# Expert weights in tiles of 2 MB, 16 KB to a partition, in a pool laid over the first part's pages

## The chip, the cores and the metric

The kernel runs on one core of a Trainium2 chip. The metric is the device time of one execution, in microseconds. The kernel before took 1446.26 us (median of three runs, 1442.34 to 1448.63). The profile is of one more execution.

## What is computed

One layer of a hybrid block over 256 latent tokens of width 1024 with a context of 256 tokens. The first part is a modulated norm, one input projection, a Fourier branch, a gated delta-rule branch, and the merge of both (`w_gdn_out`, then `w_merge_out`). The second part is a mixture of 32 experts, four of them per token, and a final norm:

```
p = u @ w_in                                   # first part, per token
x = x + g1 * ((ga * ya + gb * (yb @ w_gdn_out)) @ w_merge_out)
h2 = modulate(rmsnorm(x, norm2_g), sh2, sc2)
top 4 of 32 experts by h2 @ w_router + b_router
gate = min(h @ w_gate[e] + b_gate[e], 7);  up = clip(h @ w_up[e] + b_up[e], -7, 7)
y = ((up + 1) * gate * sigmoid(1.702 * gate)) @ w_down[e] + b_down[e]
x = x + g2 * sum over the token's experts of weight * y
out = rmsnorm(x, final_norm_g)
```

Each expert has three float32 matrices of 1024 x 1024, 4.19 MB each. All 96 of them (402.65 MB) are read once from HBM, whatever the routing.

## The kernel before

**First part.** It works in pages: 13 places of 8 KB per partition (pool `pg`) plus a pair for `x_pg` and `h2`. The projection weights go through a ring (pool `rg`, on the right side of the memory): `raw` is loaded from SP (`raw_tile`, L148), split by ScalarE into `hi` and by VectorE or GpSimd into `lo` (L156, L157), and used by three float32r matmuls (`mm3`, L164 to L166). Its last two stages are eight steps with `w_gdn_out` and eight half steps with `w_merge_out`, 512 KB of `raw` each. The last matmul of the merge reads the last `hi`.

**Expert weights.** `fetch` (L799 to L810) loads a quarter of a matrix, 1 MB, as 128 partitions with two adjacent rows each, 8 KB. Its first places are pages of `pg`; after `ring.close()` four more places (`pg2`) open over the ring, so that 17 MB fit. The table `FT` says how many loads are issued behind each `raw` load of the last two stages (one each at steps 2, 3, 7 and 14), and that 13 follow the last of them. All are issued by SP, in one queue, in the order gate 0, up 0, gate 1, up 1, down 0, gate 2, up 2, down 1 and so on.

**Experts.** `prep` gathers up to 64 tokens for two experts at a time (one-hot matmuls, L1083). `gate_up` (L1102) multiplies by gate and up: each 1 MB tile serves two of the eight steps of the contraction, with two halves of the columns on two column groups of TensorE (L1111), and a matmul for the bias ends each matrix (L1112). VectorE, ScalarE and GpSimd form the activation (L1115 to L1121), TensorE transposes it (L1124). `down` of the expert before (L1129, matmuls L1134) follows `gate_up`, so that its matmuls run beside the activation. The results are weighted, sent back to the tokens (L1141) and added (L1143). A loop for experts with over 64 tokens (L1146) stands at the end; in this data it has no turns. A TensorE matmul of the program with float32 operands is two records in the trace.

**Order.** A scheduler with a timeline model sets each engine's order from the program's order and the waits; `issue_after` adds an edge behind a given instruction. SP holds nothing but loads, issued in order, so that a load that waits holds up all behind it.

Of the kernel before, what the change touches and what calls it, by code (L numbers as in the profile page):

```python
# [10 lines left out]
F32 = mybir.dt.float32  # L11
# [13 lines left out]
NOV = 15  # L25

NPG = 13
NPG2 = 4
NEAR = 4
FT = ((0, 0, 1, 1, 0, 0, 0, 1, 0, 0, 0, 0, 0, 0, 1, 0), 13)  # L30
MODB = (0, 2, 0, 1, 1, 3, 1, 0, 2, 2, 2, 2)
EP = 1
FP = 1
# [64 lines left out]
def hybrid_block(es: ExitStack, tc: tile.TileContext, cst, x, c, ctx, c_ctx, w_mod, b_mod, norm1_g, norm2_g, w_in,  # L98
# [3 lines left out]
    V, A, G, PE, SP = nc.vector, nc.scalar, nc.gpsimd, nc.tensor, nc.sync  # L102
    mm = PE.matmul

    cp = es.enter_context(tc.tile_pool(name="cp", bufs=1))
    pg = es.enter_context(tc.tile_pool(name="pg", bufs=NPG))

    t1 = es.enter_context(ExitStack())
    tmp = t1.enter_context(tc.tile_pool(name="tmp", bufs=2))
    ring = es.enter_context(ExitStack())  # L110
    rg = ring.enter_context(tc.tile_pool(name="rg", bufs=3, side="right"))
    ps = t1.enter_context(tc.tile_pool(name="ps", bufs=1, space=PSUM))
    _nb = {"pj": 2, "pf": 2, "sc": 4}
# [5 lines left out]
    def T(tag):  # L119
        return tmp.tile([128, 512], F32, name=tag, tag=tag, bufs=_tb[tag])  # L120
# [5 lines left out]
        return tmp.tile([128, *shape], F32, name=name, bufs=1)  # L126

    def page(name, dtype=F32, tag="pg"):
        return pg.tile([128, 2048], dtype, name=name, tag=tag, bufs=NPG if tag == "pg" else 2)

    def load(src, name, tag="pg"):
        t_ = page(name, tag=tag)
# [8 lines left out]
        return ap.rearrange("p (o n) -> p o n", o=1).broadcast_to([128, a, b])  # L141


    last_raw = [None]

    def raw_tile(src):
        r = rg.tile([128, 1024], F32, name="raw", tag="raw", bufs=3)
        last_raw[0] = SP.dma_start(out=r.rearrange("p (k n) -> p k n", k=src.shape[1]), in_=src).ins  # L148
        return r

    def wsplit(src, eng, r=None):
# [640 lines left out]
        pass  # L792


    ahead, nload, pg2 = [], [0], []
    order = [(w_gate, 0), (w_up, 0)]
    for e in range(NE):
        order += [(w_gate, e + 1), (w_up, e + 1)] if e + 1 < NE else []
        order.append((w_down, e))  # L799

    def fetch(n=1):
        for _ in range(n):
            m, i = divmod(nload[0], 4)
            w, e = order[m]
            r = nload[0] - NEAR
            nload[0] += 1
            t_ = page("we") if r < 0 or r % (NPG + NPG2) >= NPG2 else pg2[0].tile([128, 2048], F32, name="we2", tag="pg2")
            t_ = t_.rearrange("p (a b) -> p a b", a=2)
            SP.dma_start(out=t_, in_=w[0, e, 256 * i:256 * i + 256, :].rearrange("(p r) n -> p r n", r=2))
            ahead.append(t_)  # L810

    def wload():
        if len(ahead) < 4:
            fetch(4 - len(ahead))
        r = ahead[:4]
        del ahead[:4]
        return r


# [26 lines left out]

    for j in range(8):
        w = wsplit(kview(w_gdn_out[0])[:, :, 128 * j:128 * j + 128], (G, V)[j % 2])
        with tc.issue_after(last_raw[0]):
            fetch(FT[0][j])  # L850
        p = P("pj")
        mm3(p[:, 0:256], [((w[0][:, k, :], w[1][:, k, :]), [y[:, k].rearrange("p c n -> p (c n)") for y in ybT]) for k in range(8)])
        mg = T("a")
        V.tensor_tensor(out=mg[:, 0:256], in0=p[:, 0:256], in1=gab[1][:, j, :], op=ALU.mult)
        V.tensor_tensor(out=mg[:, 0:256], in0=mg[:, 0:256], in1=gab[0][:, j, :], op=ALU.add)
        A.copy(mT[0][:, j, :], mg[:, 0:256])
        V.tensor_tensor(out=mT[1][:, j, :], in0=mg[:, 0:256], in1=mT[0][:, j, :].bitcast(F32), op=ALU.subtract)
# [32 lines left out]
    for g in range(4):  # L890
        p = P("pj")
        for kq in range(2):
            w = wsplit(kview(w_merge_out[0])[:, 4 * kq:4 * kq + 4, 256 * g:256 * g + 256], (G, V)[kq])
            with tc.issue_after(last_raw[0]):
                fetch(FT[0][8 + 2 * g + kq])
            for t in range(2):
                mm3(p[:, 256 * t:256 * t + 256],
                    [([m[:, 4 * kq + k, 128 * t:128 * t + 128] for m in mT], (w[0][:, k, :], w[1][:, k, :])) for k in range(4)],
                    start=(kq == 0 and t == 0), stop=(kq == 1 and t == 1))
        if g:  # L900
            logits(g - 1)
        mg = T("a")
        pv, gv = p.rearrange("p (t n) -> p t n", t=2), mg.rearrange("p (t n) -> p t n", t=2)
        gsl = slice(256 * g, 256 * g + 256)
        V.tensor_tensor(out=gv, in0=pv, in1=bc3(g1b[g // 2][:, 256 * (g % 2):256 * (g % 2) + 256], 2, 256), op=ALU.mult)
        V.tensor_tensor(out=x_pg[:, :, gsl], in0=x_pg[:, :, gsl], in1=gv, op=ALU.add)
        for t in range(2):
            A.activation(gv[:, t, :], x_pg[:, t, gsl], AF.Square, scale=1.0 / 32.0, accum_out=ss2[:, t, g:g + 1])
        V.tensor_tensor(out=h2[:, :, gsl], in0=x_pg[:, :, gsl], in1=bc3(a2b[g // 2][:, 256 * (g % 2):256 * (g % 2) + 256], 2, 256), op=ALU.mult)
    logits(3)  # L910
    ring.close()
    pg2.append(es.enter_context(tc.tile_pool(name="pg2", bufs=NPG2, side="right", reuse_waits="tile")))
    with tc.issue_after(last_raw[0]):
        fetch(FT[1])


    rs2 = smt("rs2", 2)
# [137 lines left out]
            V.tensor_tensor(out=sb_, in0=sel, in1=bc3(wt[:, t, :], NOV, 32), op=ALU.mult)  # L1055
            V.tensor_reduce(out=ov_w[:, :, t], in_=sb_, axis=AX.X, op=ALU.add)

    def rows2(k):

        o = 256 * (k // 2) + k % 2  # L1060
        return slice(o, o + 255, 2)

    last_ow, last_xg = [None], [None]

    def prep(pos, wgt, ne):

        n = 64 * ne
        oh = T("oh", 2)
        ohv = oh[:, 0:2 * n].rearrange("p (t e n) -> p t e n", t=2, e=ne)
        V.tensor_tensor(out=ohv, in0=iota.rearrange("p (a b n) -> p a b n", a=1, b=1).broadcast_to([128, 2, ne, 64]),  # L1070
                        in1=pos.rearrange("p t (e o) -> p t e o", o=1).broadcast_to([128, 2, ne, 64]), op=ALU.is_equal)
        ow = T("ow", 2)
        owv = ow[:, 0:4 * n].rearrange("p (t e b n) -> p t e b n", t=2, e=ne, b=2)
        for b in range(2):
            last_ow[0] = G.tensor_tensor(out=owv[:, :, :, b, :], in0=ohv,
                                         in1=wgt.rearrange("p t (e o) -> p t e o", o=1).broadcast_to([128, 2, ne, 64]), op=ALU.mult).ins
        xg = T("xg", 2, 512 * ne).rearrange("p (k n) -> p k n", k=8)
        for kq in range(2):
            p = Q("tp")
            for kl in range(4):  # L1080
                k = 4 * kq + kl
                for t in range(2):
                    mm(p[:, kl * n:(kl + 1) * n], h2[:, t, rows2(k)], oh[:, n * t:n * t + n], start=(t == 0), stop=(t == 1))  # L1083
            last_xg[0] = A.copy(xg[:, 4 * kq:4 * kq + 4, :], p[:, 0:4 * n].rearrange("p (k n) -> p k n", k=4)).ins

        def weights():
            wT = T("wT", 2, 256 * ne).rearrange("p (e n) -> p e n", e=ne)
            p = Q("tp")
            for e in range(ne):
                for t in range(2):  # L1090
                    PE.transpose(p[:, (2 * e + t) * 128:(2 * e + t + 1) * 128], ow[:, 2 * n * t + 128 * e:2 * n * t + 128 * e + 128], ident)
            A.copy(wT, p[:, 0:256 * ne].rearrange("p (e n) -> p e n", e=ne))
            return wT

        return xg, weights
# [7 lines left out]
    def gate_up(wgu, xg, oneh):  # L1103

        pp = []
        for b in range(2):
            p = Q("gu")
            for k in range(8):
                w = wgu[b][k // 2][:, k % 2, :]
                for g in range(2):  # L1110
                    mm(p[64 * g:64 * g + 64, :], xg[:, k, :], w[:, 512 * g:512 * g + 512], start=(k == 0), stop=False)  # L1111
            mm(p, oneh, biasr[:, 512 * b:512 * b + 512], start=False, stop=True)  # L1112
            pp.append(p)
# [7 lines left out]
        G.tensor_tensor(out=up, in0=up, in1=sg, op=ALU.mult)  # L1121
        p = Q("tp")
        for q in range(4):
            PE.transpose(p[:, q * 128:(q + 1) * 128], up[:, rows2(q)], ident)  # L1124
        aT = T("aT", 2).rearrange("p (q n) -> p q n", q=4)
        A.copy(aT, p.rearrange("p (q n) -> p q n", q=4))  # L1126
        return aT
# [1 line left out]
    def down(wd, aT, wT):  # L1129
        p = Q("dn")  # L1130
        for f in range(8):
            w = wd[f // 2][:, f % 2, :]
            for g in range(2):
                mm(p[64 * g:64 * g + 64, :], aT[:, f % 4, 64 * (f // 4):64 * (f // 4) + 64], w[:, 512 * g:512 * g + 512],  # L1134
                   start=(f == 0), stop=(f == 7))
# [9 lines left out]
    def further_blocks():  # L1145
        with tc.For_i(0, ov["n"]) as i:  # L1146
# [4 lines left out]
            V.tensor_copy(cur_[:, 4:5], ov_h[:, bass.ds(i, 1)])  # L1151

            def wfetch(w):
                ts = []
                for i in range(4):
                    t_ = page("ovw").rearrange("p (k n) -> p k n", k=2)
                    SP.dma_start(out=t_, in_=w[0, bass.ds(e, 1), 256 * i:256 * i + 256, :].rearrange("o (p r) n -> p (o r) n", r=2))
                    ts.append(t_)
                return ts

            xg, weights = prep(cur_[:, 0:2].rearrange("p (t e) -> p t e", e=1), cur_[:, 2:4].rearrange("p (t e) -> p t e", e=1), 1)
            row = tmp2.tile([128, 2], F32, name="row", bufs=1)
# [32 lines left out]
    for _ in fp:  # L1195
        pass
    w = wload()
    fng = page("fng")[:, 0:1024]
    A.dma_start(out=fng, in_=final_norm_g.rearrange("(o n) -> o n", o=1).broadcast_to([128, 1024]))
    down(w, *pend)  # L1200
    further_blocks()
# [43 lines left out]
```

## Time and profile before

| | |
|---|---|
| median of three runs | 1446.26 us |
| profiled execution, its own time | 1448.83 us |
| its span, first to last instruction | 1446.9 us |
| TensorE busy | 1303.9 us, 90% of the span |
| HBM read | 467.44 MB, of which 402.65 MB expert weights |
| last merge matmul starts; first expert matmul starts | 482.42 us; 499.67 us |

The page gives busy shares of engines, the DMA share and the rate in GB/s in 40 slices of 36 us. A busy TensorE or a busy DMA says only that there was work in flight, not that it set the end; which of two full engines is waited for is read from waits and from landings. The DMA share is the time of all packets by 16 engines, and comes out slightly over 1 where packets overlap.

### The profile page before, as it was taken

The numbers are of one execution on the slowest core, as the hardware profiler recorded it, in microseconds if no ns is written. First come the engines' busy times: TensorE is split into PE (matmuls) and PEld (weight loads), VectorE is DVE, ScalarE is ACT, GpSimd is POOL, SyncE is SP. The second block draws the span as 40 slices with busy tenths as digits, with TensorE's granted clock in tenths as the row PEclk, the third lists the DMA queues.
The fourth block names the chain that finished last, engine by engine and source line by source line (L and its number), as shares of the span: only waits on it lengthen the run. The fifth ranks groups of instructions, "written<-read, shape, count | busy, mean of one in ns | idle before, by whom it ended". The sixth has DMA issues, their size and how long they took to land. (4 is left out here: it accounts for less than half of the span.)

```text
span 1446.9 us, 18887 instructions
## 1 busy us (share of the span) xinstructions
PE 1303.9 (90%) x7761; PEld 664.9 (46%) x7761; DVE 510.8 (35%) x965; ACT 243.7 (17%) x434; POOL 276.6 (19%) x256
## 2 busy tenths in 40 slices
PE   4997859899779889999999999999999999999996
PEld 2667858578569634333333333233333333333331
DVE  3579994655348411225112111211121112111213
ACT  3443333233224200000000000000000000000001
POOL 2434336544233130000100000001000000010000
PEclk9998979999879899999999999999999999999999
DMA  9962222124336999999999999999999999999994
GB/s 323 377 249 74 73 60 75 45 78 112 88 131 223 397 406 418 420 398 419 420 421 421 421 421 421 422 420 421 421 421 421 421 421 421 422 420 421 420 422 201
DMA packets 121159, 469.74 MB, mean 325 GB/s; under 512 B 10302, under 2 KB 63782, under 8 KB 69872
## 3 DMA queue, kind: packets, MB, share of 16 engines
q1 hardware_dynamic: 119696, 466.44, 81.0%
q10 hardware_dynamic: 1088, 1.89, 0.4%
q8 instruction: 62, 1.02, 0.3%
q0 software_dynamic: 288, 0.19, 0.2%
q14 instruction: 25, 0.20, 0.0%
HBM read 467.44 MB, written 1.05 MB: 324 GB/s over the span
## 5 line engine op out<-in xcount | busy, mean ns | idle before, releaser
L1111 PE MATMUL ps_gu<-we,xg 128*64 128x512 f32 x2048 | 469.6, 598 | 0.0
L1111 PEld LDWEIGHTS ps_gu<-we,xg 128*64 128x64 f32 x2048 | 141.2, 137 | 293.4 <-issue 280.2
L1134 PE MATMUL ps_dn<-we,aT 128*64 128x512 f32 x1024 | 237.3, 600 | 0.7 <-SPq L1146 0.4
L1100 POOL CAST rowsel<-pick 128x128 fp32r<-128x128 f32 x32 | 9.7, 304 | 684.5 <-PE ps_gu L1112 684.5
L157 POOL TENSOR_TENSOR lo<-raw,hi 128x1024 fp32r<-128x1024 f32 x44 | 106.3, 2418 | 157.6 <-ACT hi L156 123.2
L1143 DVE TENSOR_TENSOR x_pg<-x_pg,ps_st 128x512 f32<-128x512 f32 x128 | 82.6, 685 | 125.7 <-PE ps_st L1141 125.7
L1134 PEld LDWEIGHTS ps_dn<-we,aT 128*64 128x64 f32 x1024 | 66.9, 136 | 120.5 <-issue 113.7
L1117 ACT ACTIVATE sg<-gt 128x512 f32<-128x512 f32 x32 | 20.1, 629 | 448.1 <-DVE gt L1115 423.6
L1119 DVE TENSOR_SCALAR up<-ps_gu 128x512 f32<-128x512 f32 x32 | 22.1, 691 | 196.0 <-PE ps_gu L1112 189.2
L1137 DVE TENSOR_TENSOR ys<-ps_dn,g2r 128x512 f32<-128x512 f32 x32 | 22.1, 692 | 195.9 <-PE ps_dn L1134 195.9
L1141 PE MATMUL ps_st<-ys,wT 64*128 64x512 f32 x256 | 77.3, 641 | 12.8 <-DVE ys L1137 12.0
L156 ACT CAST hi<-raw 128x1024 fp32r<-128x1024 f32 x64 | 66.9, 1047 | 124.5 <-PE ps_pf L165 38.1
L164 PE MATMUL ps_pj<-u,hi 128*128 128x256 f32 x224 | 68.8, 310 | 18.1 <-DVE a L391 18.1
L1126 ACT COPY aT<-ps_tp 128x512 f32<-128x512 f32 x32 | 18.8, 586 | 322.0 <-PE ps_tp L1124 322.0
L1083 PEld LDWEIGHTS ps_tp<-oh,h 128*128 128x128 f32 x512 | 64.6, 201 | 14.1 <-issue 13.3
L391 DVE SCALAR_TENSOR_TENSOR a<-ps_pj,cvw,a 128x189 f32<-128x189 f32 (+3 forms) x152 | 63.8, 432 | 18.0 <-ACT a L388 16.3
L1083 PE MATMUL ps_tp<-oh,h 128*128 128x128 f32 x512 | 68.9, 290 | 1.1 <-DVE oh L1070 1.1
L1115 DVE TENSOR_SCALAR gt<-ps_gu 128x512 f32<-128x512 f32 x32 | 22.2, 692 | 133.2 <-issue 95.4
L165 PE MATMUL ps_pj<-u,hi 128*128 128x256 f32 x224 | 68.8, 308 | 0.0
L166 PE MATMUL ps_pj<-u,lo 128*128 128x256 f32 x224 | 67.2, 301 | 0.0
L1121 POOL TENSOR_TENSOR up<-up,sg 128x512 f32<-128x512 f32 x32 | 40.4, 1263 | 96.1 <-DVE up L1120 96.1
L164 PEld LDWEIGHTS ps_pj<-u,hi 128*128 128x128 f32 x224 | 46.0, 207 | 25.6 <-issue 23.8
(352 smaller groups left out, 1663.7 us busy)
## 6 DMA issues: line engine op xcount, KB each, us to landing
we<-in_w_gate_dram SPq DMA_DIRECT2D x128, 1024.0 KB, 18.4
we<-in_w_up_dram SPq DMA_DIRECT2D x128, 1024.0 KB, 17.8
we<-in_w_down_dram SPq DMA_DIRECT2D x128, 1024.0 KB, 18.9
raw<-in_w_in_dram SPq DMA_DIRECT2D x44, 512.0 KB, 4.0
wmb<-in_w_mod_dram SPq DMA_DIRECT2D x16, 1024.0 KB, 12.8
wm<-in_w_mod_dram SPq DMA_DIRECT2D x16, 512.0 KB, 8.1
raw<-in_w_gdn_out_dram SPq DMA_DIRECT2D x8, 512.0 KB, 4.1
raw<-in_w_merge_out_dram SPq DMA_DIRECT2D x8, 512.0 KB, 3.5
```

Source lines behind the costliest of these rows:

```text
L156: A.copy(hi, r)
L157: eng.tensor_tensor(out=lo, in0=r, in1=hi.bitcast(F32), op=ALU.subtract)
L164: mm(out_, sh_, mh_, start=start and i == 0, stop=False)
L165: mm(out_, sh_, ml_, start=False, stop=False)
L166: mm(out_, sl_, mh_, start=False, stop=stop and i == n - 1)
L391: V.scalar_tensor_tensor(out=ov, in0=iv, scalar=wap, in1=ov, op0=ALU.mult, op1=ALU.add)
L1083: mm(p[:, kl * n:(kl + 1) * n], h2[:, t, rows2(k)], oh[:, n * t:n * t + n], start=(t == 0), stop=(t == 1))
L1111: mm(p[64 * g:64 * g + 64, :], xg[:, k, :], w[:, 512 * g:512 * g + 512], start=(k == 0), stop=False)
L1121: G.tensor_tensor(out=up, in0=up, in1=sg, op=ALU.mult)
L1134: mm(p[64 * g:64 * g + 64, :], aT[:, f % 4, 64 * (f // 4):64 * (f // 4) + 64], w[:, 512 * g:512 * g + 512], start=(f == 0), stop=(f == 7))
L1141: mm(p, wT[64 * g:64 * g + 64, t * 128:(t + 1) * 128], ys[64 * g:64 * g + 64, :], start=True, stop=True)
L1143: V.tensor_tensor(out=x_pg[:, t, gsl], in0=x_pg[:, t, gsl], in1=p, op=ALU.add)
```

## The change

A tile is now half a matrix: four adjacent rows per partition, 16 KB in one run, 2 MB in all (L806 in the new file, `page4`). Eight places (`NWE`, pool `we`, tags `we0` to `we7`) lie in a pool that is opened after `ring.close()` on the right side, over `rg` and `pg`, which now lie there too; `x_pg` and `h2` have a pool of their own (`pk`). The pool is opened with `reuse_waits="tile"`: a place waits for the tiles that lay beneath it. `WO` gives the tag of each load in turn. `FT` now says: one load behind the first of the last 16 `raw` loads, four behind the eighth, three behind the last. `rows4` orders the contraction's rows as the tiles hold them. The loop for further experts takes its tiles from the same places, and `fng` (the final norm's gain) lies in the tile `ov` and no longer in a page.

```diff
-NPG2 = 4
-NEAR = 4
-FT = ((0, 0, 1, 1, 0, 0, 0, 1, 0, 0, 0, 0, 0, 0, 1, 0), 13)
+NWE = 8
+WO = (7, 3, 2, 4, 5, 6, 1, 0)
+FT = ((0, 1), (7, 4), (15, 3))
...
-    pg = es.enter_context(tc.tile_pool(name="pg", bufs=NPG))
+    pk = es.enter_context(tc.tile_pool(name="pk", bufs=2))
...
+    pg = ring.enter_context(tc.tile_pool(name="pg", bufs=NPG, side="right"))
     rg = ring.enter_context(tc.tile_pool(name="rg", bufs=3, side="right"))
...
+    def page4(src):
+        t_ = we[0].tile([128, 4096], F32, name="we", tag=f"we{WO[nload[0] % NWE]}", bufs=1).rearrange("p (k n) -> p k n", k=4)
+        SP.dma_start(out=t_, in_=src)
+        nload[0] += 1
+        return t_
...
-            SP.dma_start(out=t_, in_=w[0, e, 256 * i:256 * i + 256, :].rearrange("(p r) n -> p r n", r=2))
-            ahead.append(t_)
+            ahead.append(page4(w[0, e, 512 * i:512 * i + 512, :].rearrange("(p r) n -> p r n", r=4)))
...
     ring.close()
-    pg2.append(es.enter_context(tc.tile_pool(name="pg2", bufs=NPG2, side="right", reuse_waits="tile")))
-    with tc.issue_after(last_raw[0]):
-        fetch(FT[1])
+    we.append(es.enter_context(tc.tile_pool(name="we", bufs=NWE, side="right", reuse_waits="tile")))
+    for i, n in FT:
+        with tc.issue_after(raws[i - 16]):
+            fetch(n)
...
-                w = wgu[b][k // 2][:, k % 2, :]
+                w = wgu[b][k // 4][:, k % 4, :]
...
-    fng = page("fng")[:, 0:1024]
+    fng = T("ov", 1, 1024)
```

On SP, from the end of the first part on, the kernel before has its first weight loads between the `raw` loads:

```order
L148 DMA raw<-in_w_gdn_out_dram 128x8x128 x6
L809 DMA we<-in_w_gate_dram 128x2048 x2
L148 DMA raw<-in_w_gdn_out_dram 128x8x128 x2
L809 DMA we<-in_w_gate_dram 128x2048
L148 DMA raw<-in_w_merge_out_dram 128x4x256 x7
L809 DMA we<-in_w_gate_dram 128x2048
L148 DMA raw<-in_w_merge_out_dram 128x4x256
L809 DMA we<-in_w_gate_dram 128x2048 x4
L809 DMA we<-in_w_up_dram 128x2048 x4
```

Four tiles of 1 MB stand ahead of the last `raw` load there. In the changed kernel, at the same place of SP's queue, with the semaphores that each load waits for (`PE_49`, `DVE_49`, `Pool_49` count those engines' instructions, `DMAHW0_49` to `DMAHW7_49` are eight DMA semaphores taken in turn):

```order
L150 DMA raw<-in_w_merge_out_dram 128x4x256 [waits DMAHW7_49,DVE_49]
L150 DMA raw<-in_w_merge_out_dram 128x4x256 [waits DMAHW0_49,Pool_49]
L806 DMA we<-in_w_gate_dram 128x4096 [waits DVE_49,PE_49,Pool_49]
L806 DMA we<-in_w_gate_dram 128x4096
L806 DMA we<-in_w_up_dram 128x4096 x2
L806 DMA we<-in_w_gate_dram 128x4096
L806 DMA we<-in_w_gate_dram 128x4096 [waits DMAHW1_49]
L806 DMA we<-in_w_up_dram 128x4096 [waits DMAHW2_49]
L806 DMA we<-in_w_up_dram 128x4096 [waits DMAHW3_49]
L806 DMA we<-in_w_down_dram 128x4096 [waits DMAHW4_49,PE_49]
```

No weight load stands ahead of a `raw` load any more, and the first one holds the waits for the others. In the built program its tile lies at the lowest address of the pool, over `hi` and `lo` of the ring, and the count that it wants of `PE_49` is that of the merge's last matmul (new L168, old L166), of `DVE_49` and `Pool_49` the last `lo` of each.

On TensorE, in the middle of the experts, before (`ps_gu` gate or up, `ps_dn` down of the expert before, `ps_tp` transposes, of `up` the activation):

```order
L1111 MATMUL ps_gu<-we,xg 64x512 x16
L1112 MATMUL ps_gu<-biasr,rowsel 128x512
L1134 MATMUL ps_dn<-we,aT 64x512 x4
L1124 MATMUL ps_tp<-cs,up 128x128 x4
L1091 MATMUL ps_tp<-cs,ow 128x128 x4
L1134 MATMUL ps_dn<-we,aT 64x512 x12
```

and in the changed kernel:

```order
L1112 MATMUL ps_gu<-we,xg 64x512 x16
L1113 MATMUL ps_gu<-biasr,rowsel 128x512
L1135 MATMUL ps_dn<-we,aT 64x512 x8
L1125 MATMUL ps_tp<-cs,up 128x128 x4
L1092 MATMUL ps_tp<-cs,ow 128x128 x4
L1135 MATMUL ps_dn<-we,aT 64x512 x8
```

Eight matmuls of `down` now stand between the bias matmul and the transposes, where four stood.

## Rows read from the trace of the kernel before

**Rows 1.** The page, 40 slices of the span: busy tenths of TensorE and DMA.
```profile
PE   4997859899779889999999999999999999999996
...
DMA  9962222124336999999999999999999999999994
```
**Rows 2.** Stretches: length; busy us (records) of PE, PEld, DVE, ACT, POOL; PEclk, DMA share, GB/s.
```profile
484.90:1429.60 944.70, 892.87 (x4117) 332.08 (x4118) 199.57 (x327) 69.40 (x119) 78.94 (x104) 0.99 1.01 416
...
700.00:760.00 60.00, 56.17 (x264) 20.39 (x260) 11.80 (x18) 4.09 (x7) 4.29 (x6) 1.00 1.01 421
```
**Rows 3.** Bias matmuls in two stretches: ns min/median/max, first and last start.
```profile
L1112 PE MATMUL ps_gu<-biasr,rowsel x9: 494/502/505, 710.6 to 826.2; 128*128 128x512 f32 x9
...
L1112 PE MATMUL ps_gu<-biasr,rowsel x9: 494/502/505, 1288.8 to 1404.4; 128*128 128x512 f32 x9
```
**Rows 4.** Waits of SP's queue, 700 to 1400 us: total us, times, longest.
```profile
SPq L809 <- PE ps_gu L1111: 130.0, 89, 3.4
SPq L809 <- DMA we<-in_w_up_dram: 126.0, 62, 3.7
...
SPq L809 <- PE ps_dn L1134: 89.0, 46, 5.2
```
**Rows 5.** Waits of TensorE and its weight loads, 700 to 1400 us.
```profile
PE ps_tp L1124 <- POOL up L1121: 26.9, 24, 1.1
...
PEld ps_gu L1111 <- DMA we<-in_w_down_dram: 8.2, 14, 0.8
```
**Rows 6.** The last weight loads: issues, 1395 to 1435 us, and time to landing.
```profile
L809 SPq DMA_DIRECT2D we<-in_w_down_dram x6: 327/328/328, 1396.5 to 1409.0; - x6
...
DMA to landing us min/median/max: 21.0/21.1/21.1
```
**Rows 7.** Timeline of TensorE: start, length, what, count, idle before it.
```profile
482.42 0.29 PE L166 MATMUL ps_pj<-hi,mTl 128*128 128x256 f32 x1
...
499.67 20.87 PE L1111 MATMUL ps_gu<-we,xg 128*64 128x512 f32 x96
525.27 1.65 PE L1112 MATMUL ps_gu<-biasr,rowsel 128*128 128x512 f32 x3 [4.73 <-POOL biasr L984]
...
1426.96 5.37 PE L1134 MATMUL ps_dn<-we,aT 128*64 128x512 f32 x24
```
**Rows 8.** Timeline of SP's queue, the first weight loads.
```profile
421.87 1.05 SPq L809 DMA_DIRECT2D we<-in_w_gate_dram  x2
...
465.88 0.37 SPq L148 DMA_DIRECT2D raw<-in_w_merge_out_dram  x1
466.30 2.06 SPq L809 DMA_DIRECT2D we<-in_w_gate_dram  x4
```
**Rows 9.** DMA from 424 to 485 us: packets by size; an issue, KB, us to landing.
```profile
DMA packets 8087, 16.54 MB, mean 271 GB/s; under 512 B 335, under 2 KB 6726, under 8 KB 6726
...
raw<-in_w_merge_out_dram SPq DMA_DIRECT2D x8, 512.0 KB, 3.5
```
**Rows 10.** Stretches with the columns of rows 2, around the start of the experts.
```profile
500.00:505.00 5.00, 5.00 (x26) 1.71 (x24) 0.72 (x3) 0.36 (x1) 0.99 (x2) 1.00 0.82 260
505.00:510.00 5.00, 5.00 (x26) 2.04 (x25) 0.00 (x0) 1.28 (x1) 0.49 (x1) 1.00 1.02 339
...
620.00:630.00 10.00, 10.00 (x37) 2.79 (x35) 3.46 (x5) 0.63 (x1) 0.00 (x0) 1.00 0.91 333
...
424.00:484.90 60.90, 58.43 (x436) 57.67 (x436) 39.12 (x48) 21.43 (x40) 14.65 (x6) 0.90 0.72 271
```
**Rows 11.** Stretches in which `wm` alone is loaded, in runs of 2 KB; columns of rows 2.
```profile
13.00:17.00 4.00, 1.46 (x11) 0.86 (x15) 0.51 (x2) 3.97 (x7) 0.00 (x0) 1.00 1.05 392
30.00:34.00 4.00, 4.00 (x40) 2.49 (x42) 4.00 (x11) 1.62 (x4) 2.00 (x3) 1.00 1.06 391
```
**Rows 12.** DMA issues by line: count, KB each, median us to landing.
```profile
xg<-in_b_gate_dram ACTq DMA_DIRECT2D x4, 64.0 KB, 4.0
xg<-in_b_up_dram ACTq DMA_DIRECT2D x4, 64.0 KB, 6.9
```
**Rows 13.** Timeline of ScalarE's queue, the loads of the biases.
```profile
499.83 2.23 ACTq L979 DMA_DIRECT2D xg<-in_b_gate_dram  x4
502.10 2.41 ACTq L979 DMA_DIRECT2D xg<-in_b_up_dram  x4
```

More of the change, by code (lines that the diff above doesn't have):

```diff
@@ L128, in page @@
     def page(name, dtype=F32, tag="pg"):
-        return pg.tile([128, 2048], dtype, name=name, tag=tag, bufs=NPG if tag == "pg" else 2)
+        return (pg if tag == "pg" else pk).tile([128, 2048], dtype, name=name, tag=tag, bufs=NPG if tag == "pg" else 2)
     def load(src, name, tag="pg"):
@@ L141, in bc3 @@
         return ap.rearrange("p (o n) -> p o n", o=1).broadcast_to([128, a, b])
-    last_raw = [None]
+    raws = []
     def raw_tile(src):
         r = rg.tile([128, 1024], F32, name="raw", tag="raw", bufs=3)
-        last_raw[0] = SP.dma_start(out=r.rearrange("p (k n) -> p k n", k=src.shape[1]), in_=src).ins
+        raws.append(SP.dma_start(out=r.rearrange("p (k n) -> p k n", k=src.shape[1]), in_=src).ins)
         return r
@@ L792, in hybrid_block @@
         pass
-    ahead, nload, pg2 = [], [0], []
+    ahead, nload, we = [], [0], []
     order = [(w_gate, 0), (w_up, 0)]
@@ L799, in hybrid_block @@
         order.append((w_down, e))
+    def page4(src):
[3 more added lines that the diff above has]
+        return t_
     def fetch(n=1):
         for _ in range(n):
-            m, i = divmod(nload[0], 4)
+            m, i = divmod(nload[0], 2)
             w, e = order[m]
[L805 to L808, printed above, removed]
-            SP.dma_start(out=t_, in_=w[0, e, 256 * i:256 * i + 256, :].rearrange("(p r) n -> p r n", r=2))
-            ahead.append(t_)
+            ahead.append(page4(w[0, e, 512 * i:512 * i + 512, :].rearrange("(p r) n -> p r n", r=4)))
     def wload():
[L813 to L816, printed above, removed]
+        if len(ahead) < 2:
+            fetch(2 - len(ahead))
+        r = ahead[:2]
+        del ahead[:2]
         return r
@@ L848, in hybrid_block @@
         w = wsplit(kview(w_gdn_out[0])[:, :, 128 * j:128 * j + 128], (G, V)[j % 2])
-        with tc.issue_after(last_raw[0]):
-            fetch(FT[0][j])
         p = P("pj")
@@ L893, in hybrid_block @@
             w = wsplit(kview(w_merge_out[0])[:, 4 * kq:4 * kq + 4, 256 * g:256 * g + 256], (G, V)[kq])
-            with tc.issue_after(last_raw[0]):
-                fetch(FT[0][8 + 2 * g + kq])
             for t in range(2):
@@ L911, in hybrid_block @@
     ring.close()
-    pg2.append(es.enter_context(tc.tile_pool(name="pg2", bufs=NPG2, side="right", reuse_waits="tile")))
-    with tc.issue_after(last_raw[0]):
-        fetch(FT[1])
+    we.append(es.enter_context(tc.tile_pool(name="we", bufs=NWE, side="right", reuse_waits="tile")))
+    for i, n in FT:
+        with tc.issue_after(raws[i - 16]):
+            fetch(n)
     rs2 = smt("rs2", 2)
@@ L1056, in first_part, with rows4 @@
             V.tensor_reduce(out=ov_w[:, :, t], in_=sb_, axis=AX.X, op=ALU.add)
-    def rows2(k):
-        o = 256 * (k // 2) + k % 2
-        return slice(o, o + 255, 2)
+    def rows4(k):
+        o = 512 * (k // 4) + k % 4
+        return slice(o, o + 509, 4)
     last_ow, last_xg = [None], [None]
@@ L1082, in prep @@
                 for t in range(2):
-                    mm(p[:, kl * n:(kl + 1) * n], h2[:, t, rows2(k)], oh[:, n * t:n * t + n], start=(t == 0), stop=(t == 1))
+                    mm(p[:, kl * n:(kl + 1) * n], h2[:, t, rows4(k)], oh[:, n * t:n * t + n], start=(t == 0), stop=(t == 1))
             last_xg[0] = A.copy(xg[:, 4 * kq:4 * kq + 4, :], p[:, 0:4 * n].rearrange("p (k n) -> p k n", k=4)).ins
@@ L1123, in gate_up @@
         for q in range(4):
-            PE.transpose(p[:, q * 128:(q + 1) * 128], up[:, rows2(q)], ident)
+            PE.transpose(p[:, q * 128:(q + 1) * 128], up[:, rows4(q)], ident)
         aT = T("aT", 2).rearrange("p (q n) -> p q n", q=4)
@@ L1131, in down @@
         for f in range(8):
-            w = wd[f // 2][:, f % 2, :]
+            w = wd[f // 4][:, f % 4, :]
             for g in range(2):
@@ L1153, in wfetch @@
             def wfetch(w):
[L1154 to L1159, printed above, removed]
+                return [page4(w[0, bass.ds(e, 1), 512 * i:512 * i + 512, :].rearrange("o (p r) n -> p (o r) n", r=4)) for i in range(2)]
             xg, weights = prep(cur_[:, 0:2].rearrange("p (t e) -> p t e", e=1), cur_[:, 2:4].rearrange("p (t e) -> p t e", e=1), 1)
```

## The prediction

> **What bounds the kernel now.** I read the page's 40 slices first, then the stretch of the experts, the waits there, and the last landings. From the 14th slice on both TensorE and DMA stand at nine or more tenths [rows 1]: over the experts TensorE is busy 892.9 of 944.7 us, and the DMA share is 1.01 [rows 2]. Busy shares can't tell which one is waited for, so I take the pace of each. Between two gate biases four experts apart lie 115.6 us, both at 710.6 and at 1288.8 us [rows 3]: TensorE takes 28.9 us per expert, steadily, in the middle and at the end alike. The DMA brings the 12.58 MB of an expert at 421 GB/s [rows 2] in 29.9 us. So TensorE is the faster of the two by 1.0 us per expert, and can be so only because the DMA has a lead. The waits say the same: SP waits 219 us in 135 waits for TensorE to free a place (130.0 and 89.0) and the rest for an older DMA [rows 4], while TensorE's own weight reads waited for a tile 0.8 us at the longest [rows 5]. Places are full, TensorE is the bound, and the lead is being eaten.
>
> Where does the lead end? The last tile is issued at 1409.0 and lands 21.0 us later, at 1430.0 [rows 6]. The last 24 down records run from 1426.96 to 1432.33, 0.224 us each [rows 7]; the last tile's eight begin at about 1430.5. The lead is down to half a microsecond just as the work ends. That decides this case: any lateness of the weights is paid in full from here on, and a faster TensorE would gain nothing.
>
> **The change, part by part.**
>
> *The head start.* Before, four tiles are issued among the raw loads from 421.87 on, and the rest from 466.30 [rows 8]. Now SP's first weight load waits for the merge's last matmul, and since SP issues in order, all 192 loads stand behind that wait: nothing else does, no raw load is behind it. That matmul starts at 482.42 and is done at 482.7 [rows 7]. First bytes follow some 2.2 us later: a raw load of 512 KB needs 1.25 us at 421 GB/s and lands after 3.5 [rows 9]. So the stream begins at 484.9. By then the kernel before had moved 1361 packets of 8 KB or more [rows 9], 11.1 MB of weights, worth 26.4 us at 421 GB/s. Can the first part end sooner without this traffic? TensorE is busy 58.4 of its last 60.9 us [rows 10], so hardly: 0 to 2 us, taken as 0. **+26.4 us**, between 24 and 27.
>
> *Stalls that go.* Before, all 17 places are full when TensorE starts at 499.67, and the DMA falls to 260 and 339 GB/s for 5 us each, later to 333 for 10 us [rows 10]. Against 421 that is 0.81, 0.41 and 0.88 MB, 5.0 us. With eight places filling only until 484.9 + 16.78 MB at 421 = 524.8, and the first one freed by about 503 (16 records of 0.217 us from 499.67 on, rows 7), the new queue has no such stall. **-5.0 us**, between 0 and -5. New waits for places stand no closer than seven tiles, 35 us, behind the landing; TensorE lags by two or three tiles, so I put them at 0. The ninth to seventeenth loads wait besides for the DMA semaphores of the bias loads, which ScalarE issues at 499.83 to 504.5 and which land after 4.0 to 6.9 us [rows 12, 13]. Those must land before the eighth tile, at 524.8; beside a full weight queue they may take twice or three times as long and still do. Cover gone, each microsecond past it costs one.
>
> *Run length.* This is the unknown: no weight packet of 16 KB is in the trace. The nearest rows are the 2 KB runs, at 391.5 GB/s with the engines full (share 1.05) [rows 11], and the 8 KB runs, at 421 (share 1.01) [rows 2]. Per engine, a sixteenth of that, a packet takes 83.7 ns and 311.3 ns. A straight line through both is 37.04 ns per KB of 1000 bytes and 7.8 ns fixed, so 16 KB takes 614.7 ns: 426.5 GB/s. The 402.65 MB take 944.1 us in place of 956.4: **-12.3 us**. Ends: no gain at all (421), 0; no fixed cost left (432.0), -24.3. I take the line, since both its rows are loads from the same memory to the same one.
>
> [...]
>
> *Last tile.* When the last landing comes, 16 records are left where eight were: 8 x 0.224 = **+1.8 us**. What follows it (the last projection, the final norm, the output) is unchanged.
>
> *TensorE.* Eight matmuls of down now cover the activation where four did, and the wait of 1.1 us for GpSimd ahead of the transposes [rows 5] should shrink. TensorE's pace falls below 28.9 us per expert, which is worth nothing now: the DMA at 426.5 GB/s needs 29.5. It will wait for tiles from about 530 us on, a microsecond or so at a time, as long as the waits that it has in the experts now at full clock [rows 2, 5]. The row selection (rows4), the pool for x_pg and h2, the loop without turns and the place of fng change no instruction's size: 0.
>
> *Sum:* +26.4 - 5.0 - 12.3 + 1.8 = **+10.9 us**. The profiled execution, 1448.83 us with a span of 1446.9, becomes 1459.7. It lies 2.6 us above the median of the runs, so I expect 1446.26 + 10.9, **1457 us**.
>
> **The rivals.**
>
> *Half the gain of the run length.* At 2 KB the loads come from SP in 512 KB pieces, and part of what they lack against 421 may be the issue and not the packet; with half of the fixed cost the gain is 6.2 us: +17.0, 1463. For it: the same stretch is the start of the kernel, with other loads about. Against it: the DMA share there is 1.05, so the engines did not wait. [...]
>
> *No gain.* A 16 KB run is moved as smaller pieces inside, at the pace of now: +23.2, 1469. Nothing in the trace speaks for a limit at 421 but its evenness.
>
> *The other side: not slower.* What holds 421 back is all per-packet cost, and long runs hide it wholly. The place is the weight stream after 484.9. At 432.0 GB/s, the line without its fixed part, the sum is -1.1: 1445. From 428.3 GB/s on the change is no longer slower by more than 0.5%, at 431.5 it is even. For it: packets overlap, as the share of 1.01 says, and a longer packet leaves more to hide under. Against it: so did the 8 KB ones, and still lost.
>
> *The change does what its tables say.* Were five tiles on their way among the merge, 10.5 MB of the 11.1 would be back and the sum would be -14: 1432. The built order is against it: the first load's wait for the last merge matmul stands in the program, with all others behind.
>
> **How the numbers follow.** Forecast 0.52, half the gain 0.14, no gain 0.10, other side 0.18, early loads 0.04, and 0.02 for something slower (the bias loads, or a clock that drops in TensorE's waits). The forecast's own range is 1452 to 1463, from 424.5 to 428.5 GB/s and the 2 us left open in the head start. The range of 1446 to 1468 takes in the forecast and half the gain, about half of no gain and half of the other side, and leaves out the early loads and what remains of both, under 0.2. A change under 0.5%, 7.2 us, can't be told from none here. Slower by more: 0.43 of the forecast, both smaller gains and the last 0.02, 0.69; within: 0.09 of the forecast and 0.16 of the other side, 0.25; faster: 0.06.
>
> **What would show it.** SP's first weight load at about 482.8 us, right behind the last merge matmul, and no weight packet before 484; DMA in the experts without the dips at 500 and 620; a rate of 426 to 427 GB/s in the middle; TensorE waiting for tiles in most experts, with an expert every 29.5 us and not 28.9; the last landing at about 1438 and 3.6 us of down behind it. A rate at 421 or above 430 decides between the rivals. If TensorE shows a reduced clock in the experts, or SP waits for places while fewer than six tiles are in flight, the reasoning is wrong in its bound and not in a size.

## Result, and the profile after

The changed kernel takes 1499.2 us, the median of 4 runs (1494.37 to 1506.42), against 1446.45 for the kernel before on the same chip: a ratio of 1.037, with a 95% interval from 1.032 to 1.042. The prediction had the sign right (slower) and the size wrong: 10.9 us forecast, 52.8 measured, well above the range. The profiled execution is the slowest of the four, 1506.42 us with a span of 1504.5; what follows is measured within it, 57.6 us of span above the one before.

The page of the changed kernel, busy tenths of TensorE and DMA in 40 slices:

```profile
PE   4997769999698769999899999999999999999996
...
DMA  9952223033244999999999999999999999999990
```

Stretches of the same kernel, with the columns of [rows 2]:

```profile
484.90:1429.60 944.70, 897.46 (x3874) 374.75 (x3874) 186.24 (x305) 66.11 (x112) 75.94 (x102) 0.98 0.99 412
700.00:760.00 60.00, 55.44 (x236) 23.09 (x236) 10.50 (x16) 4.09 (x7) 4.30 (x6) 0.97 0.98 406
...
515.00:530.00 15.00, 6.44 (x31) 1.84 (x26) 0.00 (x0) 0.74 (x1) 2.35 (x4) 0.81 1.01 402
600.00:620.00 20.00, 20.00 (x71) 5.79 (x72) 6.80 (x11) 1.00 (x2) 0.86 (x2) 1.00 1.01 428
620.00:640.00 20.00, 20.00 (x90) 11.45 (x88) 3.23 (x4) 1.76 (x3) 0.71 (x1) 1.00 0.88 370
```

Against [rows 1, 2] TensorE is as full as before, and the DMA is less so: 406 GB/s from 700 to 760 us, where it had 421. It did 428 from 600 to 620 us. So it is not the transfers that became slower. The pace, from the records of the bias matmuls as in [rows 3], says who did:

```profile
L1113 PE MATMUL ps_gu<-biasr,rowsel x9: 495/502/505, 737.7 to 858.7; 128*128 128x512 f32 x9
```

Four experts lie 121.0 us apart where they lay 115.6: 30.25 us each instead of 28.9, although the forecast had TensorE getting quicker. SP's waits, 700 to 1400 us (total us, times, longest):

```profile
SPq L806 <- PE ps_gu L1112: 379.8, 92, 6.1
SPq L806 <- PE ps_dn L1135: 263.4, 46, 11.3
```

In [rows 4] 219 us of them fell to TensorE and the rest to older transfers; now all 643 us fall to TensorE, and TensorE's own waits for weights are gone from the list of its waits. SP's list alone would not decide it: in the kernel with both mends (a sorted h2 and the biases on another queue, below), where the weights do bind, 612 of 642 us fall to TensorE too. The time from issue to landing decides. Two lines of the changed kernel's page (KB each, median us):

```profile
we<-in_w_gate_dram SPq DMA_DIRECT2D x64, 2048.0 KB, 13.6
we<-in_w_down_dram SPq DMA_DIRECT2D x64, 2048.0 KB, 13.0
```

and one of the kernel with both mends:

```profile
we<-in_w_down_dram SPq DMA_DIRECT2D x64, 2048.0 KB, 32.8
```

At 427 GB/s (measured there) a tile of 2 MB takes 4.9 us. So two or three tiles are in flight in the changed kernel, and the other places hold tiles that TensorE has yet to read; with both mends some seven are in flight. The changed kernel waits for TensorE. What is longer in TensorE is above all one group. Here it is in the kernel before (busy us, mean ns of one; idle before):

```profile
L1083 PEld LDWEIGHTS ps_tp<-oh,h 128*128 128x128 f32 x512 | 64.6, 201 | 14.1 <-issue 13.3
...
L1083 PE MATMUL ps_tp<-oh,h 128*128 128x128 f32 x512 | 68.9, 290 | 1.1 <-DVE oh L1070 1.1
```

and after:

```profile
L1084 PE MATMUL ps_tp<-oh,h 128*128 128x128 f32 x512 | 122.5, 398 | 1.1 <-DVE oh L1071 1.1
L1084 PEld LDWEIGHTS ps_tp<-oh,h 128*128 128x128 f32 x512 | 120.8, 328 | 2.8 <-issue 2.0
```

These are the gather's 512 matmuls with a slice of h2 as the stationary operand. Count and shape are the same; only the distance between neighbours in the slice changed, from two floats (rows2) to four (rows4). A weight load goes from 201 to 328 ns, and the matmul record beside it from 290 to 398. A pair's 32 records take 7.6 us where they took 4.2, and 16 times 3.4 is 54 us.

A smaller group is longer too, the matmuls that send the results back to the tokens, before and after:

```profile
L1141 PE MATMUL ps_st<-ys,wT 64*128 64x512 f32 x256 | 77.3, 641 | 12.8 <-DVE ys L1137 12.0 <-DVE x_pg L1143 0.8
L1142 PE MATMUL ps_st<-ys,wT 64*128 64x512 f32 x256 | 89.6, 641 | 22.9 <-DVE ys L1138 12.0 <-DVE x_pg L1144 10.8
```

They now wait 10.8 us for VectorE's additions to `x_pg` instead of 0.8. The runs below that keep the changed kernel's order on TensorE have this too, those with the order of before have not; the order was not tried by itself.

The second difference is at the start. TensorE of the changed kernel in time order (start, length, what, count, idle before it):

```profile
500.62 20.82 PE L1112 MATMUL ps_gu<-we,xg 128*64 128x512 f32 x96
541.06 1.65 PE L1113 MATMUL ps_gu<-biasr,rowsel 128*128 128x512 f32 x3 [19.62 <-POOL biasr L985]
```

ScalarE and its queue at that time (this fence), and SP's queue (the next one):

```profile
500.79 4.94 ACTq L980 DMA_DIRECT2D xg<-in_b_gate_dram  x4
511.99 16.76 ACTq L980 DMA_DIRECT2D xg<-in_b_up_dram  x4
528.79 0.43 ACTq L981 DMA_DIRECT2D ov<-in_b_down_dram  x1
529.25 1.28 ACT L1118 ACT_TABLE_LOAD   x1 [27.94 <-DMA xg<-in_b_up_dram]
```

```profile
481.81 0.82 SPq L806 DMA_DIRECT2D we<-in_w_gate_dram  x2
...
484.84 0.96 SPq L806 DMA_DIRECT2D we<-in_w_up_dram  x2
507.99 4.33 SPq L806 DMA_DIRECT2D we<-in_w_down_dram  x2
```

In [rows 7, 13] the first bias matmul stood at 525.27 after 4.73 us of idling, and the eight bias loads were issued within 5 us of each other. Now the second four are spread over 17 us, and TensorE idles 19.6 us. SP's first weight load is where the forecast had it, at 481.81, with its first packet at 482.8.

### The profile page after: what moved, and what is told of

Same layout as the page of the kernel before. It is cut to its first block, busy times and chain, and to the rows that moved or that the text cites. A ratio compares the mean times of both kernels' runs of the same rounds, so it can differ in the third digit from the quotient of the medians.

```text
span 1504.5 us, 18507 instructions
## 1 busy us (share of the span) xinstructions
PE 1368.4 (91%) x7761; PEld 729.3 (48%) x7761; DVE 513.4 (34%) x965; ACT 244.2 (16%) x434; POOL 275.2 (18%) x256
## 5 line engine op out<-in xcount | busy, mean ns | idle before, releaser
L1112 PE MATMUL ps_gu<-we,xg 128*64 128x512 f32 x2048 | 464.8, 597 | 0.0
L1084 PE MATMUL ps_tp<-oh,h 128*128 128x128 f32 x512 | 122.5, 398 | 1.1 <-DVE oh L1071 1.1
L1084 PEld LDWEIGHTS ps_tp<-oh,h 128*128 128x128 f32 x512 | 120.8, 328 | 2.8 <-issue 2.0
L1142 PE MATMUL ps_st<-ys,wT 64*128 64x512 f32 x256 | 89.6, 641 | 22.9 <-DVE ys L1138 12.0
L166 PE MATMUL ps_pj<-u,hi 128*128 128x256 f32 x224 | 69.4, 313 | 17.3 <-DVE a L393 17.3
L168 PE MATMUL ps_pj<-u,lo 128*128 128x256 f32 x224 | 67.9, 304 | 1.0 <-issue 1.0
L1142 PEld LDWEIGHTS ps_st<-ys,wT 64*128 64x128 f32 x256 | 23.9, 184 | 78.5 <-issue 30.3
L166 PEld LDWEIGHTS ps_pj<-u,hi 128*128 128x128 f32 x224 | 46.9, 211 | 25.7 <-issue 24.9
```

The source lines that it names most:

```text
L166: mm(out_, sh_, mh_, start=start and i == 0, stop=False)
L168: mm(out_, sl_, mh_, start=False, stop=stop and i == n - 1)
L1084: mm(p[:, kl * n:(kl + 1) * n], h2[:, t, rows4(k)], oh[:, n * t:n * t + n], start=(t == 0), stop=(t == 1))
L1142: mm(p, wT[64 * g:64 * g + 64, t * 128:(t + 1) * 128], ys[64 * g:64 * g + 64, :], start=True, stop=True)
```

## The experiments

They stand by subject. Eight floats apart, fewer bias loads, two runs of 8 KB and the places by number were put on record after the results of the other four. Times are medians; the kernel before ran beside them at 1445.4 and 1445.7 us.

**The stride alone, in the kernel before.** Only the gather's slices change:

```
-  mm(p[..], h2[:, t, rows2(k)], oh[..], ..)      # every 2nd float
+  mm(p[..], h2[:, t, rows4(k)], oh[..], ..)      # every 4th float
```

> The kernel before, in which only the gather's slices of h2 are taken four floats apart instead of two (the rows of the weights still lie two to a partition, so the sums no longer pair with their weights and the output is not the reference's; nothing else is changed). Theory A, the stride of the weights that TensorE loads costs the time: LDWEIGHTS of the gather goes from 201 to about 328 ns, its matmuls from 290 to about 398, a pair's gather from 4.2 to 7.6 us, so 16 times 3.4 = 54 us of TensorE, of which the waits of 1.1 us before each transpose of up (32 of them, some 24 to 27 us) may swallow up to 25: 1475 to 1500 us. Theory B, the longer gather of the changed kernel comes from something else in it (the places, the 16 KB packets beside it, a lower granted clock): LDWEIGHTS stays near 201 ns and the time at 1446 +- 4 us.

Measured: 1500.2 us (ratio 1.038, 1.033 to 1.043), the time of the changed kernel, with places, transfers and order of the kernel before. Its weight loads:

```profile
L1088 PEld LDWEIGHTS ps_tp<-oh,h 128*128 128x128 f32 x512 | 121.8, 328 | 14.1 <-issue 13.3 <-ACT xg L1089 0.8
```

Theory A, 0.2 us above its upper end: the stride makes the same 328 ns, and the waits ahead of the transposes did not shrink to pay for it (29.4 us in all, as before). Pairs lie 61.5 us apart instead of 57.8.

**Eight floats apart**, one execution, the same edit with `slice(k, k + 1017, 8)`.

> The kernel before with the gather's slices eight floats apart (32 bytes; the output is not the reference's, as with four). Theory A (TensorE's loading of weights slows in proportion to the distance): LDWEIGHTS near 580 ns and the time near 1600 us. Theory B (one step between 8 and 16 bytes, and no further): LDWEIGHTS near 328 ns and 1500 us.

Measured: 1508.3 us, 334 ns a weight load. Theory B: for the gather, with 199 ns at one float (next experiment), 201 at two, 328 at four and 334 at eight there is one step, between 8 and 16 bytes. Why it lies there is not shown. Another stationary operand, at the end of this document, does not pay for 16 bytes (207 and 210 ns).

**The changed kernel with a sorted h2.** The four DVE instructions that finish h2 write its columns in the order of the gather into a second tile; no instruction is added:

```
+  hp = hpp.tile([128, 2048], ..)                 # 8 KB beside the places
-  stt(out=hv, in0=hv, ..)
+  stt(out=hp[..].rearrange("p (a r n) -> p a n r", r=4), in0=hv.rearrange("p (a n r) -> p a n r", r=4), ..)
-  mm(p[..], h2[:, t, rows4(k)], ..)
+  mm(p[..], hp[:, t, 128 * k:128 * k + 128], ..)
```

> The changed kernel, with h2 written by the same four instructions of DVE into a second tile with its columns sorted, so that the gather's slices are 128 neighbours. Theory A (the stride costs it): LDWEIGHTS falls from 328 to about 190 ns, that of the other loads of neighbours, a pair's gather from 7.6 to 4.2 us or less, and the time by 30 to 54 us, to 1445 to 1469; it cannot fall further than the weights allow, which start at 482.8 us and at 427 GB/s need 944 us. Theory B (the gather lies beside other waits, and the places or the transfers set the pace): 1494 to 1504 us.

Measured: 1454.3 us (ratio 1.007, 1.005 to 1.010), 44.9 less than the changed kernel.

```profile
L1087 PEld LDWEIGHTS ps_tp<-oh,hp 128*128 128x128 f32 x512 | 61.4, 199 | 2.8 <-issue 2.0 <-ACT xg L1088 0.8
```

Theory A. TensorE's pairs are 56.6 us apart until about 1200 us, quicker than before, and 58.8 to 59.0 from 1265 us on: there the weights have become the bound.

**The biases on another queue**, the gather left strided. The nine loads are issued by GpSimd, ahead of its work for the first pair:

```
-  A.dma_start(out=braw[r, ..], in_=src[0, :, ..])
+  G.dma_start(out=braw[r, ..], in_=src[0, :, ..])   # traced before the first pair
```

> The changed kernel, with the nine loads of the biases issued by GpSimd on its own queue, ahead of its work for the first pair, instead of by ScalarE behind it. Theory A (the nine loads wait for the semaphores that the first eight weight loads hold, so each waits until one of those has landed, and the weight loads behind them wait in turn): the biases land by about 505, the first bias matmul comes at about 525 us instead of 541, as in the kernel before, SyncE waits no more for a load of biases, and the time falls by 13 to 18 us, to 1481 to 1486. Theory B (the biases are slow because their packets share 16 engines with a full weight queue): they land little earlier relative to their issue (9 and 6 us), the bias matmul comes at 535 or later, and the time stays within 6 us of 1499.

Measured: 1487.6 us (1485.63 to 1487.92), 11.6 below the changed kernel, 1.4 short of the expected fall and nearer to theory A than to B. The two profiled spans, 1483.7 and 1504.5, lie 20.8 apart, of which 5.8 stand ahead of the first gather, so in the first part. In time order on TensorE:

```profile
514.07 3.65 PE L1117 MATMUL ps_gu<-we,xg 128*64 128x512 f32 x16 [1.26 <-DMA we<-in_w_gate_dram]
517.65 0.97 PE L1118 MATMUL ps_gu<-biasr,rowsel 128*128 128x512 f32 x3
519.06 3.65 PE L1117 MATMUL ps_gu<-we,xg 128*64 128x512 f32 x16 [0.44 <-DMA we<-in_w_up_dram]
```

The biases stop nothing any more, and TensorE waits here for the first weights instead. Among SP's waits for a transfer there is no bias load left. The edit does two things, though: the loads take other semaphores, and they are issued at 479.4 to 485.9 us instead of 500.8 to 528.8. What held them can be read in the changed kernel itself: the program gives the loads from SP's and ScalarE's queues eight semaphores in turn, and the first eight weight loads hold all of them. By the packets' records the fifth to the eighth of these landed at 511.4, 517.1, 522.5 and 527.9 us. The four bias loads of up were issued at 511.99, 517.71, 523.09 and 528.43. Each went 0.5 to 0.6 us after the weight load whose semaphore it takes, and 0.02 us after that semaphore's last count (511.97, 517.69, 523.07, 528.41). Once issued they were not slow (KB each, median us to landing; 4.0 and 6.9 in [rows 12]):

```profile
xg<-in_b_gate_dram ACTq DMA_DIRECT2D x4, 64.0 KB, 9.1
xg<-in_b_up_dram ACTq DMA_DIRECT2D x4, 64.0 KB, 6.2
```

**Fewer bias loads.** The same bytes in place, by half as many loads, each of which reads its 32 rows twice:

```
-  for part in range(2): A.dma_start(out=braw[r, ..], in_=src[0, :, ..])          # 32 partitions
+  A.dma_start(out=braw[64 * g:64 * g + 64, ..], in_=src[:, :, ..].broadcast_to([2, 32, 512]))
```

> The changed kernel, where ScalarE loads the biases at the same place of its program, the same bytes in four loads and one instead of eight and one (both halves by one load that reads the rows twice). Theory A (each load waits for one of the semaphores that the weight loads hold, in turn): with four fewer the last of them waits for the fourth weight load instead of the eighth, the bias matmul comes at 523 to 528 us instead of 541, and the time falls by 11 to 17 us, to 1483 to 1489. Theory B (the packets of the biases are slow among those of the weights): the bytes are the same, so the bias matmul stays within 4 us of 541 and the time at 1494 to 1504.

Measured: 1531.5 us, slower by 32: a miss of both theories, and of the experiment as a test. A second thing had changed with it. ScalarE's queue in time order:

```profile
501.11 1.20 ACTq L978 DMA_DIRECT2D xg<-in_b_gate_dram  x2
502.35 20.40 ACTq L978 DMA_DIRECT2D xg<-in_b_up_dram  x2
522.79 20.35 ACTq L980 DMA_DIRECT2D ov<-in_b_down_dram  x1
```

Its loads left 24 completion records of 4 bytes instead of 144. The nine loads of the changed kernel left 16 each, so I read 24 as 16 for the down biases and two for each of the four others. The 64 packets of such a load start two at a time, 0.6 to 0.7 us apart, as if each stood behind one of 16 KB. 32 times the 614 ns of such a packet is 19.6 us; the first load's two records come 21 us behind its first packet. That the four ran on two engines, 32 packets on each, is my estimate from these numbers; the trace does not name an engine. So what fewer loads are worth was not tested by itself. The issue did come as theory A had it, the last of the four at 505.42, behind the fourth weight load's last count at 505.39. The point on the semaphores rests on such times, and its price on the run with GpSimd's queue.

**Both mends together**, the sorted h2 and the biases on GpSimd's queue.

> The changed kernel with both: the sorted copy of h2 for the gather, and the biases on GpSimd's queue. Theory A (the two are the two errors of the prediction, and its other terms hold: later first load, faster long rows): 1457 us, between 1446 and 1468, and TensorE then waits for weights near the end of the program. Theory B (something else of the change costs time as well, such as the places opened in a fixed order): above 1468. Theory C (the transfers no longer bind at all, the parts simply add up: 1499 - 54 - 15): 1430 us.

Measured: 1457.2 us (1449.18 to 1461.65, 10 runs; ratio 1.009, 1.006 to 1.011). Theory A. That it fits to the microsecond is luck: the ten runs spread over 12 us. Waits of TensorE, 700 to 1400 us:

```profile
PE ps_gu L1120 <- DMA we<-in_w_up_dram: 11.8, 12, 1.2
...
PE ps_dn L1143 <- DMA we<-in_w_down_dram: 9.1, 10, 0.9
```

Stretches of the stream (length, PEclk, DMA share, GB/s):

```profile
490.00:600.00 110.00, 0.97 1.01 417
600.00:800.00 200.00, 0.99 1.01 426
800.00:1000.00 200.00, 1.00 1.01 427
```

From 850 to 1324 us pairs lie 59.2 us apart in the mean, 29.6 us an expert where the prediction said 29.5, TensorE waits for a tile a microsecond at a time, and the weights end at 1435.5 (said: 1438). With the bias stall (1454.3) or without it (1457.2) the time is the same within the spread: once the weights bind, 15 us of TensorE at the start are worth nothing.

**Two runs of 8 KB in each place**, otherwise the kernel with both mends (the stride is two floats again, so no sorted copy is needed).

```
-  w[..].rearrange("(p r) n -> p r n", r=4)
+  w[..].rearrange("(a p r) n -> p a r n", a=2, r=2)
```

> The kernel with the biases mended, its places of 2 MB and their order untouched, but each partition takes twice two adjacent rows (two runs of 8 KB) instead of four (one run of 16 KB), by the same number of DMAs; the gather then goes by a stride of two floats, which needs no sorted copy. Theory A (the length of the run sets the rate, as the prediction had it): packets of 8,192 bytes, 421 GB/s in stretches where the queue is full instead of 427, and the time is 12 us above that of the kernel with both mends: 1469 (1464 to 1474). Theory B (the run length is worth nothing here): 1453 to 1461.

Measured: 1470.5 us (ratio 1.017, 1.015 to 1.018), 13.3 above the kernel with 16 KB runs. Theory A. The same stretches:

```profile
490.00:600.00 110.00, 0.98 1.01 411
600.00:800.00 200.00, 0.99 1.01 420
800.00:1000.00 200.00, 1.00 1.01 420
```

Packets of 16,384 bytes take 614 ns, those of 8,192 bytes 313 (medians).

**The places in the order of their numbers.** Both mends, and eight pools of one place each, so that the first loads lie over pages that are free early:

```
-  we = pool(bufs=8, side="right")          # placed in order of first use
+  for i in range(8): we.insert(0, pool(bufs=1, side="right"))
```

> The kernel with both mends, and the eight places opened one by one from the top down, so that the first loads lie over pages that are read for the last time before the merge, instead of over the ring that the merge reads. Theory A (the weights' delivery sets the pace from the first load to the end, so a load that starts earlier ends the program earlier): the first weight load is issued at about 462.5 us, behind the last load of the ring, instead of 478 to 482; with 16 to 20 us of head start the time falls from 1457 to about 1437 (1433 to 1443), under the kernel before. Theory B (the head start is spent on waits: the places are full, or the loads slow the last loads of the merge): 1448 to 1460.

Measured: 1443.1 us (ratio 0.997, 0.995 to 0.998): 0.3% under the kernel before, and 14.1 below both mends instead of 20. SP's queue:

```profile
463.16 0.97 SPq L806 DMA_DIRECT2D we<-in_w_gate_dram  x2
464.18 1.00 SPq L806 DMA_DIRECT2D we<-in_w_up_dram  x2
465.22 13.79 SPq L806 DMA_DIRECT2D we<-in_w_gate_dram  x2
```

That is 0.1 us outside the range of theory A and 5 from that of B. Theory A holds with a smaller head start: the first packet comes at 465.5 instead of 479.3, 13.8 us. The expectation took 16 to 20, and for 1437 the upper end; that counts from 482.8, where the changed kernel's stream begins, and that of both mends begins 3.5 us sooner. This is the best version found. Its gain on the kernel before lies inside the 0.5% that this document counts as no change, though its interval excludes 1.

## Why the prediction was wrong

*Right.* The first load at 482 us behind the last merge matmul; the run length, forecast as 614.7 ns a packet and 12.3 us, measured as 614 ns and 13.3 us; that the stalls for full places go, but only once the weights bind: 420 to 431 GB/s from 600 to 660 us with both mends, while the changed kernel has its dip from 630 to 640 (316 GB/s) and a new one beside the bias loads, 505 to 515. With 427 GB/s in the middle, the three rivals on the rate are settled. The doubled run brings 1.7% (427 against 420).

*The step that failed* is the one sentence "The row selection (rows4) ... change no instruction's size: 0". It counts instructions and their shapes, and both are unchanged; but the stride of the gather's operand was part of its cost (a weight load of 201 ns at two floats, 328 at four). It was mis-sized by 54 us of TensorE. The 41 us that the stretch from the second expert to the last grew by are this: 15 pairs by 2.7 us. By the starts of TensorE's matmuls, a steady pair has 3.5 us more in the gather, 2.5 less up to the transposes, where the waits went as the prediction had it, and 1.9 more in sending results back, which it left out; the rest is 0.2 less. TensorE's pace did not fall below 28.9 us, though with the sorted h2 it does (56.6 us a pair is 28.3). And so the bound was wrong: the sum was one of the weights' stream, while the changed kernel waits for TensorE all along. The prediction's own test, SP waiting for places with fewer than six tiles in flight, says so: there are two or three.

*The second error* is the bias loads. They were given the right dependence in one direction (weight loads nine to seventeen wait for the bias loads) and not in the other (the bias loads wait for the first eight). "Two or three times as long and still do" treated their lateness as a slow transfer; it was a late issue, the last load of up 24 us behind that of the kernel before. TensorE idles 15 us more for it, of the first 18 us lost up to the second expert, and, as TensorE was the bound, most of it stayed in the time: the run without it is 11.6 us faster. By itself it would not have put the forecast wrong, for with the sorted h2 it costs nothing.

*What this says of the sum.* With both errors mended the kernel takes 1457.2 us, the number forecast. The head start, the run length and the wait for the last tile therefore hold as a sum. Not each alone: the stream began at 479.3 in that kernel, 5.6 us before the forecast's 484.9. The first packet comes 1.0 us behind the last merge matmul, where 2.2 were taken, and that matmul starts at 478.0 where 482.4 was: in the six profiled executions with all weights behind it, it starts at 475.6 to 481.8, in the three with some ahead at 481.1 to 485.5, so the first part does seem to end sooner, which was taken as 0. Against that, the stream's average from first to last packet, 402.65 MB in 956.2 us, is 421 GB/s where 427 was measured in the middle; it loses some 13 us beside the biases and at its ends. The forecast kept such losses by starting from the stream of before, which had 391.5 MB in 945.1 us, 414 GB/s. The forecast's own range, from the rates that it names and 2 us less head start, comes out at 1451 to 1462, not 1452 to 1463; nothing hangs on it.

## What to carry over

A layout changed for the DMA changes the stride at which some other engine reads: follow each index function to all its uses, and price an operand by the bytes between neighbours as well as by its shape (the gather's weight load took 201 ns at 8 bytes and 328 at 16, that of the transposes 207 and 210). A small load that shares semaphores in turn with large ones is issued when the large ones land, however short it is itself (here 0.02 us behind their last counts, at 511.99 to 528.43 us, where the kernel before issued them from 502.10 to 504.5); put it ahead of them or on a queue that takes other semaphores. And where two engines are within a few per cent of each other (here 28.9 and 29.9 us an expert), a forecast needs the pace of both after the change, since the one that was not worked out becomes the bound.

## What was not expected of the hardware

A weight load of the gather, 128 x 128 floats, takes 199, 201, 328 and 334 ns with neighbours 4, 8, 16 and 32 bytes apart. The transposes of `up`, whose slices went from 8 to 16 bytes by the same change, kept 207 and 210 ns; why these do not pay is open.

Beside the bias loads, 0.66 MB in all, the core's whole DMA traffic, biases counted, falls from 427 to 346 GB/s for 15 us at a DMA share of 1.03, in the kernel with the places by number (stretch, PEclk, DMA share, GB/s), and to 351 to 376 in the changed one, 505 to 515 us:

```profile
485.00:500.00 15.00, 0.61 1.03 346
```

That is 2.8 us of traffic lost, on top of the 1.5 us that the biases' own bytes are worth: the weights alone had 303 GB/s there. What the 2.8 us are was not tried.
